# A two-layer decoder trunk on one Trainium2 core: reordering the expert stage's index work, one-hots, four late tiles and gate products

## The chip, the cores and the metric

The kernel runs on one core of a Trainium2 chip. The metric is device time in microseconds (us), from the start to the end of one execution; the profile beside it is one execution of the same program.

## The reference

Two layers. Each has a mixer (a gated linear recurrence beside a sparse attention) and then the PEER expert stage, which the change touches:

```python
q = (xf @ wq).reshape(T, 8, 2, 128)                       # T = 256 tokens, 8 heads
s = jnp.einsum('thcd,ckd->thck', q, subkeys)
sv, si = lax.top_k(s, 16)                                 # top 16 of 128 keys, for both halves
cand = sv[:, :, 0, :, None] + sv[:, :, 1, None, :]        # 16 x 16 sums
cv, ci = lax.top_k(cand.reshape(T, 8, 256), 16)           # top 16 pairs
ea = take_along_axis(si[:, :, 0], ci // 16, axis=-1)
eb = take_along_axis(si[:, :, 1], ci % 16, axis=-1)
experts = ea * 128 + eb                                   # 128 of 16384 experts per token
gate = softmax(cv)
act = gelu(einsum('cd,ced->ce', x, u_tab[experts]))       # rows of 1024
y = einsum('ce,ced->cd', act * gate, v_tab[experts])
x = layer_norm(ALPHA * x + y)
```

## The kernel before

The kernel does not gather rows. It multiplies every token with all 16384 rows of both tables, 128 tiles of 128 rows each, and uses a dense matrix G of gates (128 rows a tile, zero where a token did not choose the expert).

A table tile comes through `wtile` (L95 to L107): SyncE loads 512 KB into `raw` (4 buffers), ScalarE casts it to `hi` (L102, 3 buffers), and VectorE, or GpSimd for the first 14 u tiles (`NPOOL`), takes the remainder `lo` = raw - hi (L103, 3 buffers). TensorE multiplies in three terms, hi·hi, lo·hi and hi·lo. A **u tile** is 24 matmuls (L111); every second one ends in a Gelu on ScalarE into an `act` tile (4 buffers, `NACT`) that is written to DRAM (`kept`). A **v tile** is 12 matmuls (L983).

One layer's expert stage runs through three parts:

- **Index work.** u tiles run on TensorE while VectorE does the top-k. The generator `work()` yields the VectorE cost of each step, and u tiles are put in as that cost adds up. Per head: `query` (a product with wq, copied by ScalarE at L780), scores (L797), `top` (20 VectorE instructions). Per half of the heads (g is 0 or 1): `pairs` (sums `cd`, L811, and their best 16) and `choices` (an Exp on ScalarE, L834, and 26 steps with the tiles `sif`, `ge` and `t` that turn the chosen pairs into indices and gates). `turn_round` transposes the result (L882).
- **One-hots.** 32 steps: two VectorE instructions make one-hot tiles `ohg` for 8 tokens (L934, L938), 16 matmuls (L945) and four ScalarE copies (L949) put their gates into G. The other u tiles lie between.
- **Second pass.** For each pair of v tiles: `fetch` brings an act tile back on SyncE's queue (L965), `w_pair` multiplies it with G on VectorE (L961), `w_split` casts it (ScalarE L974) and takes the remainder (VectorE L975) into `W8`, and the v tiles are multiplied. Near its end, the rows of the layer norm, five or three v tiles and, in the first layer, weights of the next one are loaded ahead.

The framework keeps each engine's queue in order, and its scheduler may move an instruction ahead of program order where its inputs allow; `tc.keep_in_program_order` pins one. The lines to follow are these:

Of the kernel before, what the change touches and what calls it, by code (L numbers as in the profile page):

```python
# [47 lines left out]
ROOT_ACT = {1, 2, 3}  # L48
NACT = 4
NPOOL = 14  # L50
NCAND = 50
CNT = [16 // (i + 1) for i in range(16)]
OFF = [sum(CNT[:i]) for i in range(16)]
# [23 lines left out]
def trunk_kernel(ctx: ExitStack, tc: tile.TileContext, x, xt, cst, lam, pvec, brow, w_in, w_lx, w_v, w_q4, lru_w,  # L77
# [187 lines left out]
    for l in range(NL):  # L265
# [3 lines left out]
        with tc.tile_pool(name="mix", bufs=1, reuse_waits="tile") as mp, \  # L269
# [196 lines left out]
            def gates(qb, br, h0, h1):  # L466
                return vrow[:, qb, 256 + br * 8 + h0:256 + br * 8 + h1]
# [259 lines left out]
        with tc.tile_pool(name="peer", bufs=1, reuse_waits="tile") as pp:  # L727
# [10 lines left out]
            def u_tile(a):  # L738
                if a % 2 == 0:
                    ub[a] = bank()  # L740
                ps = ub[a - a % 2]
                col_mm(ps[:, HALF[a % 2]], wtile(u_tab[l, a], (8, 128), POOL if a < NPOOL else DVE), xT)
                if a % 2:
                    at = act_tile()
                    ACT.activation(at.rearrange("p a b -> p (a b)"), ps, AF.Gelu_apprx_tanh)  # L745
                    kept[a - 1] = spill.tile([128, 2, S], F32, name="kept%d" % (a - 1), bufs=1)
                    ACT.dma_start(kept[a - 1], at)

            with tc.tile_pool(name="topk", bufs=1, reuse_waits="tile") as tk:
# [141 lines left out]
                def work():  # L891
                    for h in (2, 0, 1, 3):
                        yield from top(h)
                    yield from pairs(0)
                    yield from choices(0)
                    for h in range(4, 8):
                        query(h)
                        yield 2.44 - 5.76
                        yield from top(h)
                    yield from pairs(1)  # L900
                    yield from choices(1)
                    yield 0.0
                    yield from turn_round()

                for h in (2, 0, 1, 3):
                    if h == 0:
# [10 lines left out]
            with tc.tile_pool(name="dense", bufs=1, reuse_waits="tile") as dp:  # L917
# [10 lines left out]
                def onehots(t0):  # L928

                    ohg = (state.tile([128, 2, 4, 2, 128, 2], F16, tag="xTf", name="ohg") if t0 % 16 else  # L930
                           pp.tile([128, 2, 4, 2, 128, 2], F16, name="ohg"))
                    oh, og = ohg[:, 0], ohg[:, 1]
                    qs = slice(t0 // 2, t0 // 2 + 4)
                    DVE.tensor_tensor(oh.rearrange("p q w a i -> p (q w) a i"),  # L934
                                      iota.unsqueeze(1).to_broadcast([128, 8, 128, 2]),
                                      eT[:, qs].rearrange("p q w i -> p (q w) i").unsqueeze(2).to_broadcast([128, 8, 128, 2]),
                                      op=ALU.is_equal)
                    DVE.tensor_tensor(og, oh[:, :, 0:1].to_broadcast([128, 4, 2, 128, 2]),  # L938
                                      gT[:, qs].unsqueeze(3).to_broadcast([128, 4, 2, 128, 2]), op=ALU.mult)
                    for h in range(2):  # L940
                        ps = bank()
                        for k in range(4):
                            q, i = divmod(4 * h + k, 2)
                            for w in range(2):
                                PE.matmul(ps[:, k * 128:k * 128 + 128], oh[:, q, 1, :, i], og[:, q, w, :, i],  # L945
                                          start=w == 0, stop=w == 1)
                        t1 = t0 + 4 * h
                        for g in range(2):
                            ACT.activation(G[g][:, :, t1:t1 + 4],  # L949
                                           ps.rearrange("p (t g a) -> p g a t", g=2, a=64)[:, g], AF.Copy, scale=1.0 / GSC)  # L950

                a0 = a
                for i in range(32):
                    onehots(8 * i)
                    while a < 128 and (a - a0) * 32 < (i + 1) * (128 - a0):
                        u_tile(a)
                        a += 1
                assert a == 128

                def w_pair(a0):  # L960
                    DVE.tensor_tensor(act[a0], act[a0], G[a0 // 64][:, a0 % 64:a0 % 64 + 2, :], op=ALU.mult)  # L961

                def fetch(a0):
                    act[a0] = act_tile()
# [87 lines left out]
                for j in range(2):  # L1052
                    ready(j)
                w_pair(body[0])
                for j, p in enumerate(body):
                    ready(j + 2)
                    ready(j + 3)
                    v_tile(p)
                    w_pair(seq[j + 1])
                    v_tile(p + 1)  # L1060
                    step[0] = j
                    left = len(body) - j
                    if left == 16:
                        gb = ln_gb(new_gb, (l, 0))
                        for tb in range(2):
                            ln_affine(gb, tb)
                    if left <= 14 and pre:
                        f, i = pre.pop(0)
                        f(i)
                        if left <= len(pre):  # L1070
                            f, i = pre.pop(0)
                            f(i)
# [193 lines left out]
```

## Time and profile before

| | us |
|---|---|
| median of 3 runs (lowest to highest) | 1985.06 (1984.7 to 1985.13) |
| profiled execution | 1986.41 |
| span of its trace, first to last instruction | 1984.6 |
| TensorE busy in it | 1910.3 (96%) |
| VectorE busy | 1322.8 (67%) |
| ScalarE busy | 976.4 (49%) |
| GpSimd busy | 82.0 (4%) |

The table says which engine has the least idle time over the whole span; it does not say where in the span its idle time lies. PE is TensorE, PEld its weight loads, DVE VectorE, ACT ScalarE, POOL GpSimd, SP SyncE. Most runs of this kernel lie within 0.3% of one another.

### The profile page before, as it was taken

Reading aid. Unit: us, or ns where it says so; the run is one execution under the profiler, and the core shown is the slowest. Engines: PE = TensorE matmul, PEld = TensorE weight load, DVE = VectorE, ACT = ScalarE, POOL = GpSimd, SP = SyncE. Lnnn points to the kernel's source line nnn. Section 1 sums busy time; section 2 is a strip of 40 time slices with the busy share of each in tenths; the row PEclk is TensorE's granted clock in tenths of the full one; section 3 lists DMA queues with packets and bytes.
Section 4 is the critical chain, followed back from the end, with each engine's and each line's share of the span. In section 5 each row is a group of like instructions: output and inputs, shape, how many; then the busy total and the mean of one; then the engine's idle time right before and its main releaser. Section 6 shows DMA issues by size and latency. Waiting matters only on the chain.

```text
span 1984.6 us, 32589 instructions
## 1 busy us (share of the span) xinstructions
PE 1910.3 (96%) x12580; PEld 1681.0 (85%) x12580; DVE 1322.8 (67%) x2553; ACT 976.4 (49%) x1579; POOL 82.0 (4%) x55
## 2 busy tenths in 40 slices
PE   8999899999999999999999998999999989999998
PEld 7858899999998888777868488999999988887876
DVE  5664878666665666657667639786666656667666
ACT  3635444455554555445446344444555545555553
POOL 0005200000000000000000052000000000000000
PEclk9999999999999999999999999999999999999999
DMA  8405547566666777778553056575666657778783
GB/s 276 155 0 180 195 160 234 177 199 207 199 202 215 241 241 242 248 255 278 175 182 106 0 169 188 161 237 175 205 201 203 206 199 254 239 244 264 244 264 117
DMA packets 130096, 393.92 MB, mean 198 GB/s; under 512 B 15634, under 2 KB 16404, under 8 KB 129812
## 3 DMA queue, kind: packets, MB, share of 16 engines
q1 hardware_dynamic: 111508, 358.28, 56.2%
q10 hardware_dynamic: 18432, 33.56, 4.6%
q8 instruction: 98, 1.61, 0.3%
q14 instruction: 58, 0.48, 0.1%
HBM read 357.18 MB, written 34.60 MB: 197 GB/s over the span
## 4 chain that ended last, share of the span: by engine, by line
PE 80%; DMA 9%; DVE 6%; issue 2%; ACT 1%; POOL 0%; SPq 0%; POOLq 0%; DVEq 0%; ACTq 0%
PE ps L111 41%; PE ps L983 25%; DMA act<-kept 6%; PE ps L945 3%; PE ps L589 3%; PE ps L118 2%; DVE lo L103 2%; DMA raw<-in_v_tab_dram 1%; PE ps L231 1%; PE ps L797 1%; PE ps L561 1%; PE ps L514 1%; DVE W L975 1%; PE ps L369 0%; POOL lo L103 0%
## 5 line engine op out<-in xcount | busy, mean ns | idle before, releaser
L102 ACT CAST hi<-raw 128x1024 fp32r<-128x1024 f32 x548 | 575.4, 1051 | 483.5 <-PE ps L111 413.2
L103 DVE TENSOR_TENSOR lo<-raw,hi 128x1024 fp32r<-128x1024 f32 x516 | 629.6, 1222 | 267.3 <-ACT hi L102 266.8
L111 PE MATMUL ps<-xThi,hi 128*128 128x256 f32 x2400 | 692.0, 288 | 6.5 <-ACT hi L102 6.5
L111 PE MATMUL ps<-xThi,lo 128*128 128x256 f32 x2400 | 683.5, 285 | 8.3 <-POOL lo L103 6.0
L111 PE MATMUL ps<-xTlo,hi 128*128 128x256 f32 x2400 | 682.8, 285 | 0.0
L983 PE MATMUL ps<-hi,W 128*128 128x512 f32 x1936 | 523.1, 392 | 10.2 <-ACT W L974 10.0
L111 PEld LDWEIGHTS ps<-xThi,lo 128*128 128x128 f32 x2400 | 463.6, 193 | 10.6 <-POOL lo L103 6.9
L111 PEld LDWEIGHTS ps<-xThi,hi 128*128 128x128 f32 x2400 | 464.1, 193 | 7.9 <-ACT hi L102 6.9
L111 PEld LDWEIGHTS ps<-xTlo,hi 128*128 128x128 f32 x2400 | 464.1, 193 | 0.3
L983 PEld LDWEIGHTS ps<-hi,W 128*128 128x128 f32 x1936 | 365.9, 189 | 88.6 <-ACT W L974 10.4
L983 PE MATMUL ps<-lo,W 128*128 128x512 f32 x968 | 302.6, 394 | 13.1 <-DVE lo L103 12.9
L983 PEld LDWEIGHTS ps<-lo,W 128*128 128x128 f32 x968 | 180.7, 189 | 59.5 <-DVE lo L103 23.2
L974 ACT CAST W<-act 128x256 fp32r<-128x256 f32 x242 | 97.7, 407 | 266.2 <-PE ps L983 258.2
L961 DVE TENSOR_TENSOR act<-act,G 128x512 f32<-128x512 f32 x128 | 88.4, 692 | 172.9 <-DMA act<-kept 170.3
L975 DVE TENSOR_TENSOR W<-act,W 128x256 fp32r<-128x256 f32 x242 | 101.0, 420 | 10.3 <-PE ps L983 8.1
L103 POOL TENSOR_TENSOR lo<-raw,hi 128x1024 fp32r<-128x1024 f32 x32 | 78.5, 2460 | 315.5 <-ACT hi L102 315.5
L949 ACT ACTIVATE G<-ps 128x256 f32<-128x256 f32 x256 | 80.3, 383 | 12.2 <-PE ps L945 8.2
L938 DVE TENSOR_TENSOR ohg<-ohg,gT 128x2048 f16<-128x2048 f16 x64 | 78.2, 1225 | 2.1
L945 PE MATMUL ps<-ohg 128*128 128x128 f16 x1024 | 71.5, 222 | 8.2 <-DVE ohg L938 8.2
L934 DVE TENSOR_TENSOR ohg<-iota,eT 128x2048 f16<-128x2048 f16 x64 | 77.9, 1220 | 1.7 <-PE ps L945 1.7
L745 ACT ACTIVATE act<-ps 128x512 f32<-128x512 f32 x128 | 75.6, 591 | 0.1
L945 PEld LDWEIGHTS <-ohg 128*128 128x128 f16 x1024 | 60.3, 98 | 11.3 <-DVE ohg L938 8.6
(256 smaller groups left out, 1186.6 us busy)
## 6 DMA issues: line engine op xcount, KB each, us to landing
raw<-in_u_tab_dram SPq DMA_DIRECT2D x256, 512.0 KB, 3.6
raw<-in_v_tab_dram SPq DMA_DIRECT2D x256, 512.0 KB, 4.5
kept<-act ACTq DMA_DIRECT2D x128, 256.0 KB, 2.5
act<-kept SPq DMA_DIRECT2D x128, 256.0 KB, 3.8
raw<-in_w_in_dram SPq DMA_DIRECT2D x24, 512.0 KB, 4.3
raw<-in_wq_dram SPq DMA_DIRECT2D x24, 512.0 KB, 4.3
ow<-in_w_out_dram SPq DMA_DIRECT2D x16, 512.0 KB, 7.9
qf<-in_w_q_dram SPq DMA_DIRECT2D x8, 512.0 KB, 3.8
```

The source lines that it names most:

```text
L102: ACT.copy(hi, raw)
L103: lo_eng.tensor_tensor(lo, raw, hi, op=ALU.subtract)
L111: PE.matmul(ps, a[m], b[n], start=start and i == 0, stop=stop and i == 2)
L745: ACT.activation(at.rearrange("p a b -> p (a b)"), ps, AF.Gelu_apprx_tanh)
L934: DVE.tensor_tensor(oh.rearrange("p q w a i -> p (q w) a i"), iota.unsqueeze(1).to_broadcast([128, 8, 128, 2]), eT[:, qs].rearrange("p q w ...
L938: DVE.tensor_tensor(og, oh[:, :, 0:1].to_broadcast([128, 4, 2, 128, 2]), gT[:, qs].unsqueeze(3).to_broadcast([128, 4, 2, 128, 2]), op=ALU. ...
L945: PE.matmul(ps[:, k * 128:k * 128 + 128], oh[:, q, 1, :, i], og[:, q, w, :, i], start=w == 0, stop=w == 1)
L949: ACT.activation(G[g][:, :, t1:t1 + 4], ps.rearrange("p (t g a) -> p g a t", g=2, a=64)[:, g], AF.Copy, scale=1.0 / GSC)
L961: DVE.tensor_tensor(act[a0], act[a0], G[a0 // 64][:, a0 % 64:a0 % 64 + 2, :], op=ALU.mult)
L974: ACT.copy(whi, at[:, a % 2])
L975: DVE.tensor_tensor(wlo, at[:, a % 2], whi, op=ALU.subtract)
L983: PE.matmul(accs[tb * 2 + hf], ww[m][:, TB[tb]], v[n][:, hf * 512:hf * 512 + 512], start=a == first[0] and (m, n) == (0, 0), stop=a == 127 ...
```

## The change

Five edits in the expert stage. In `work()`, `choices(0)` is written after `pairs(1)`, the query of a head is written a head earlier, the costs yielded around them change and the last step yields 4.0 after `turn_round`. The one-hot loop makes the one-hots of a step ahead of the u tiles of the step before, and `gates` (the matmuls and copies) follows them. The last four u tiles (`NLATE`) run after the first two fetches and the first `w_pair` of the second pass. And `w_pair` is pinned to program order.

```diff
--- before.py
+++ after.py
@@ -48,6 +48,7 @@
 ROOT_ACT = {1, 2, 3}
 NACT = 4
 NPOOL = 14
+NLATE = 4
 NCAND = 50
 CNT = [16 // (i + 1) for i in range(16)]
 OFF = [sum(CNT[:i]) for i in range(16)]
@@ -892,15 +893,19 @@
                     for h in (2, 0, 1, 3):
                         yield from top(h)
                     yield from pairs(0)
-                    yield from choices(0)
+                    query(4)
+                    yield 2.44 - 5.76
                     for h in range(4, 8):
-                        query(h)
-                        yield 2.44 - 5.76
+                        if h < 7:
+                            query(h + 1)
+                            yield 2.44 - 5.76
                         yield from top(h)
                     yield from pairs(1)
+                    yield from choices(0)
                     yield from choices(1)
-                    yield 0.0
+                    yield 1.0
                     yield from turn_round()
+                    yield 4.0
 
                 for h in (2, 0, 1, 3):
                     if h == 0:
@@ -937,6 +942,10 @@
                                       op=ALU.is_equal)
                     DVE.tensor_tensor(og, oh[:, :, 0:1].to_broadcast([128, 4, 2, 128, 2]),
                                       gT[:, qs].unsqueeze(3).to_broadcast([128, 4, 2, 128, 2]), op=ALU.mult)
+                    return oh, og
+
+                def gates(t0, oh, og):
+
                     for h in range(2):
                         ps = bank()
                         for k in range(4):
@@ -950,15 +959,18 @@
                                            ps.rearrange("p (t g a) -> p g a t", g=2, a=64)[:, g], AF.Copy, scale=1.0 / GSC)
 
                 a0 = a
+                made = onehots(0)
                 for i in range(32):
-                    onehots(8 * i)
-                    while a < 128 and (a - a0) * 32 < (i + 1) * (128 - a0):
+                    following = onehots(8 * i + 8) if i < 31 else None
+                    while a < 128 - NLATE and (a - a0) * 32 < (i + 1) * (128 - NLATE - a0):
                         u_tile(a)
                         a += 1
-                assert a == 128
+                    gates(8 * i, *made)
+                    made = following
 
                 def w_pair(a0):
-                    DVE.tensor_tensor(act[a0], act[a0], G[a0 // 64][:, a0 % 64:a0 % 64 + 2, :], op=ALU.mult)
+                    i = DVE.tensor_tensor(act[a0], act[a0], G[a0 // 64][:, a0 % 64:a0 % 64 + 2, :], op=ALU.mult)
+                    tc.keep_in_program_order(i)
 
                 def fetch(a0):
                     act[a0] = act_tile()
@@ -1052,6 +1064,8 @@
                 for j in range(2):
                     ready(j)
                 w_pair(body[0])
+                for a in range(128 - NLATE, 128):
+                    u_tile(a)
                 for j, p in enumerate(body):
                     ready(j + 2)
                     ready(j + 3)
```

Where this puts things in the queues can be read at three places. The first is VectorE's queue in the index work of the first layer, before, from the end of the best 16 of `pairs(0)` on; `gt`, `cif`, `ge` and `t1` belong to `choices(0)`, `lo_2106` and `lo_2138` to table tiles:

```order
L833 TENSOR_TENSOR gt_2015<-cv_1363 128x128
L843 CAST cif_2022<-ci_1364 128x128
L850 TENSOR_TENSOR ge_2061<-cif_2022,i16_131 128x2048
L871 TENSOR_REDUCE gs_2016<-gt_2015 128x8
L854 TENSOR_TENSOR t1_2097<-ge_2061,dsi_2020 128x2048
L859 TENSOR_TENSOR t1_2134<-ge_2061,dst_2021 128x2048
L825 TENSOR_TENSOR t1_2097<-t1_2097 128x128x8
L103 TENSOR_TENSOR lo_2106<-raw_2104,hi_2105 128x1024
L825 TENSOR_TENSOR t1_2097<-t1_2097 128x128x4
```

The same place after the change; `lo_2049`, `lo_2082` and `lo_2112` belong to the queries of heads 4 and 5:

```order
L834 TENSOR_TENSOR gt_2784<-cv_1363 128x128
L844 CAST cif_2791<-ci_1364 128x128
L851 TENSOR_TENSOR ge_2833<-cif_2791,i16_131 128x2048
L104 TENSOR_TENSOR lo_2049<-raw_2047,hi_2048 128x1024
L855 TENSOR_TENSOR t1_2866<-ge_2833,dsi_2789 128x2048
L104 TENSOR_TENSOR lo_2082<-raw_2080,hi_2081 128x1024
L826 TENSOR_TENSOR t1_2866<-t1_2866 128x128x8
L860 TENSOR_TENSOR t1_2971<-ge_2833,dst_2790 128x2048
L104 TENSOR_TENSOR lo_2112<-raw_2110,hi_2111 128x1024
```

`choices(0)` still stands right behind `pairs(0)`, since the scheduler brings it forward, and the remainders of two more query tiles stand between its steps. Between its large product (L868 before, L869 after) and the first sum `cd` of the second `pairs` stand the best 16 of four heads and, before, 18 remainders; after the change 5, and the first remainder behind these sums is lo_2550. From the best 16 of `pairs(0)` to lo_2550 there are 11 remainders in all.

The second place is SyncE's queue at the boundary between the passes, before; the act tiles are the fetches for the first v tiles:

```order
L100 DMA raw_7033<-in_u_tab_dram 128x1024
L100 DMA raw_7063<-in_u_tab_dram 128x1024
L100 DMA raw_7113<-in_v_tab_dram 128x1024
L100 DMA raw_7134<-in_v_tab_dram 128x1024
L100 DMA raw_7156<-in_v_tab_dram 128x1024
L100 DMA raw_7177<-in_v_tab_dram 128x1024
L100 DMA raw_7199<-in_v_tab_dram 128x1024
L100 DMA raw_7220<-in_v_tab_dram 128x1024
L965 DMA act_7098<-kept0_1545 128x512
L965 DMA act_7100<-kept2_1638 128x512
L965 DMA act_7103<-kept4_1731 128x512
```

And after the change:

```order
L101 DMA raw_7039<-in_u_tab_dram 128x1024
L101 DMA raw_7069<-in_u_tab_dram 128x1024
L101 DMA raw_7113<-in_v_tab_dram 128x1024
L101 DMA raw_7134<-in_v_tab_dram 128x1024
L977 DMA act_6968<-kept0_1545 128x512
L977 DMA act_6970<-kept2_1638 128x512
L101 DMA raw_7156<-in_v_tab_dram 128x1024
L101 DMA raw_7177<-in_v_tab_dram 128x1024
L101 DMA raw_7199<-in_v_tab_dram 128x1024
L101 DMA raw_7220<-in_v_tab_dram 128x1024
L977 DMA act_7103<-kept4_1731 128x512
```

The first two fetches moved from behind six loads of v tiles to behind two. In the one-hot stage, which is not shown, six u tiles stand on TensorE between `turn_round` and the first one-hot matmuls after the change, and none before.

The third place is VectorE's queue in the second pass, before:

```order
L975 TENSOR_TENSOR W8_7097<-act_7152,W8_7097 128x256
L103 TENSOR_TENSOR lo_7265<-raw_7263,hi_7264 128x1024
L961 TENSOR_TENSOR act_7281<-act_7281,G_3565 128x512
L975 TENSOR_TENSOR W8_7097<-act_7152,W8_7097 128x256
L103 TENSOR_TENSOR lo_7287<-raw_7285,hi_7286 128x1024
L975 TENSOR_TENSOR W8_7097<-act_7195,W8_7097 128x256
L961 TENSOR_TENSOR act_7324<-act_7324,G_3565 128x512
L103 TENSOR_TENSOR lo_7308<-raw_7306,hi_7307 128x1024
L975 TENSOR_TENSOR W8_7097<-act_7195,W8_7097 128x256
L103 TENSOR_TENSOR lo_7330<-raw_7328,hi_7329 128x1024
```

And after the change, at the same tiles:

```order
L972 TENSOR_TENSOR act_7105<-act_7105,G_3661 128x512
L104 TENSOR_TENSOR lo_7222<-raw_7220,hi_7221 128x1024
L987 TENSOR_TENSOR W8_6967<-act_7105,W8_6967 128x256 x2
L104 TENSOR_TENSOR lo_7244<-raw_7242,hi_7243 128x1024
L972 TENSOR_TENSOR act_7152<-act_7152,G_3661 128x512
L104 TENSOR_TENSOR lo_7265<-raw_7263,hi_7264 128x1024
L987 TENSOR_TENSOR W8_6967<-act_7152,W8_6967 128x256 x2
L104 TENSOR_TENSOR lo_7287<-raw_7285,hi_7286 128x1024
L972 TENSOR_TENSOR act_7195<-act_7195,G_3661 128x512
L104 TENSOR_TENSOR lo_7308<-raw_7306,hi_7307 128x1024
```

Before, `w_pair` of act_7281 stood ahead of the splits of act_7195 and act_7238; after, each `w_pair` stands with one remainder between it and its own pair's splits, a pair ahead of that pair's matmuls.

## Rows read from the trace of the kernel before

**Rows 1.** The page: busy times, and the chain that ended last.

```profile
PE 1910.3 (96%) x12580; PEld 1681.0 (85%) x12580; DVE 1322.8 (67%) x2553; ACT 976.4 (49%) x1579; POOL 82.0 (4%) x55
...
PE ps L111 41%; PE ps L983 25%; DMA act<-kept 6%; PE ps L945 3%; PE ps L589 3%; PE ps L118 2%; DVE lo L103 2%; DMA raw<-in_v_tab_dram 1%; PE ps L231 1%; PE ps L797 1%; PE ps L561 1%; PE ps L514 1%; DVE W L975 1%; PE ps L369 0%; POOL lo L103 0%
```

**Rows 2.** The chain: start, length, what held it (a u tile; second pass).

```profile
42.47 2.87 PE ps L111 x24
...
626.05 154.99 PE ps L983 x672
```

**Rows 3.** Ten stretches: length, busy times, granted clock, DMA share, GB/s.

```profile
208.00:340.00 132.00, 122.56 (x994) 120.80 (x993) 109.55 (x345) 59.45 (x70) 3.31 (x1) 0.97 0.60 195
1203.50:1336.00 132.50, 122.93 (x994) 121.27 (x993) 109.44 (x345) 59.45 (x70) 3.31 (x1) 0.97 0.61 195
340.00:353.00 13.00, 8.91 (x61) 8.68 (x60) 8.79 (x10) 3.90 (x7) 0.00 (x0) 0.74 0.34 102
1336.00:1349.00 13.00, 8.92 (x71) 8.68 (x70) 9.93 (x10) 3.90 (x7) 0.00 (x0) 0.87 0.32 103
618.00:632.00 14.00, 9.12 (x43) 7.69 (x42) 7.52 (x12) 4.98 (x9) 0.00 (x0) 0.76 0.73 240
1613.00:1627.00 14.00, 8.85 (x45) 7.50 (x44) 6.87 (x11) 5.47 (x9) 0.00 (x0) 0.88 0.68 239
632.00:785.00 153.00, 153.00 (x677) 126.67 (x676) 105.37 (x140) 82.41 (x113) 0.00 (x0) 1.00 0.72 235
785.00:905.00 120.00, 112.71 (x480) 89.89 (x479) 75.17 (x106) 57.76 (x80) 0.00 (x0) 0.99 0.80 256
905.00:960.00 55.00, 51.74 (x217) 39.71 (x216) 40.05 (x55) 29.04 (x44) 0.00 (x0) 1.00 0.83 275
1790.00:1912.00 122.00, 119.24 (x521) 96.89 (x520) 85.12 (x117) 64.77 (x89) 0.00 (x0) 1.00 0.80 259
```

**Rows 4.** Waits over the whole span: total, times, longest.

```profile
ACT gt L834 <- DVE gt L833: 14.9, 2, 7.4
...
PE ps L945 <- DVE ohg L938: 8.2, 2, 4.1
```

**Rows 5.** Timeline of PE, 256 to 275: start, length, [idle before, releaser].

```profile
259.51 1.16 PE L797 MATMUL ps<-skt,qh 128*128 128x128 f32 x8 [1.50 <-ACT qh L780]
260.42 0.37 PE L111 MATMUL ps<-xThi,hi 128*128 128x256 f32 x1
```

**Rows 6.** Timeline of DVE, 198 to 312.

```profile
203.84 2.49 DVE L842 CAST sif<-si 128x256 f16<-128x256 uint32 x1
...
215.72 3.17 DVE L854 TENSOR_TENSOR t<-ge,dsi 128x2048 f16<-128x2048 f16 x1
...
251.59 0.49 DVE L784 MAX8 sv<-ss 128x8 f32<-128x128 f32 x2 [1.09 <-ACT ss L799]
...
255.63 0.28 DVE L786 MATCH_REPLACE8 s<-sv,ss 128x128 f32<-128x128 f32 x1
...
304.32 0.27 DVE L842 CAST sif<-si 128x256 f16<-128x256 uint32 x1
...
309.71 1.22 DVE L854 TENSOR_TENSOR t<-ge,dsi 128x2048 f16<-128x2048 f16 x1
```

**Rows 7.** Timeline of POOL, 195 to 330.

```profile
214.50 3.31 POOL L103 TENSOR_TENSOR lo<-raw,hi 128x1024 fp32r<-128x1024 f32 x1 [8.32 <-ACT hi L102]
```

**Rows 8.** One stretch more, 204 to 258, columns as in rows 3.

```profile
204.00:258.00 54.00, 47.98 (x381) 47.13 (x379) 45.42 (x136) 22.57 (x28) 5.49 (x2) 0.94 0.56 181
```

**Rows 9.** SyncE's queue, 600 to 640: start, length, what it issued.

```profile
604.18 16.68 SPq L100 DMA_DIRECT2D raw<-in_v_tab_dram  x6
```

**Rows 10.** The page's groups of DVE: busy, mean ns | idle before.

```profile
L103 DVE TENSOR_TENSOR lo<-raw,hi 128x1024 fp32r<-128x1024 f32 x516 | 629.6, 1222 | 267.3 <-ACT hi L102 266.8
...
L961 DVE TENSOR_TENSOR act<-act,G 128x512 f32<-128x512 f32 x128 | 88.4, 692 | 172.9 <-DMA act<-kept 170.3
```

**Rows 11.** DMA issues of the page, KB each, us to landing.

```profile
act<-kept SPq DMA_DIRECT2D x128, 256.0 KB, 3.8
```

## The prediction

> **What bounds the kernel now.** Start with the page. TensorE is busy for 1910.3 of 1984.6 us, and the chain that ended last runs mostly through u tiles (41%) and v tiles (25%) [rows 1]. Busy time on another engine is therefore worth nothing by itself, and the change can win at most what TensorE loses. Next come the unit prices from the chain: a u tile takes 2.87 us, and 672 v matmuls take 154.99, so a v tile of 12 takes 2.77 and a pair 5.54 [rows 2]. The view of stretches then says where the loss lies [rows 3]. In 632 to 785 TensorE is never idle, at full clock, so the middle of the second pass has nothing to give. The other stretches lose time in two ways, idle time and a granted clock under 1.00. For each I take the stretch less PE's busy time, and add (1 - clock) times the busy time, or times the whole stretch where the idle pieces are short:
>
> - Index work, 208 to 340: 132 - 122.56 = 9.4 idle, and 0.03 x 132 = 4.0 of clock, together 13.4. In the second layer 9.6 and 4.0, 13.6.
> - Start of the one-hots, 340 to 353: 4.1 idle and 0.26 x 8.91 = 2.3, together 6.4. Second layer 4.1 and 1.2, 5.3.
> - Boundary of the passes, 618 to 632: 4.9 and 0.24 x 9.12 = 2.2, together 7.1. Second layer 5.15 and 1.1, 6.2.
> - End of the second pass: the undisturbed stretch does 677 matmuls in 153 us, 0.226 each. By that the 480 + 217 from 785 to 960 are worth 157.5 of 175 us, a loss of 17.5, and in the second layer 521 are worth 117.7 of 122, a loss of 4.3.
>
> These sum to 73.8 us. The sums are made against the profiled execution, 1986.41; the median of the runs is 1.35 below it, so I take differences and subtract them from 1985.06. A measurement of this kernel can tell about 0.2% (4 us) from no change.
>
> **A. Index work.** What is to go is a wait for an Exp: ScalarE stood for 7.4 us behind the instruction of VectorE that feeds it, once in each layer [rows 4], with the casts of table tiles queued behind. The two waits of 1.50 us for a copied query (one of them in [rows 5]) go too, since the query comes a head earlier. But the order of the queues shows that `choices(0)` stays where it was and that query remainders now lie between its steps. Behind it the best 16 of all four heads come together, with 5 remainders between them where there were 18. So VectorE becomes the bound. Up to lo_2550 it has the work that it did from 204 to 258, 45.4 us [rows 8], with three more heads. Of a head's 20 instructions, 18 take from 251.59 to 255.91 [rows 6], 4.3 us, so a head takes 4.8 and three take 14.4. Two remainders fewer at 1.22 [rows 10] take off 2.4, and the sums of the second `pairs` add 1.3 (an estimate from their nine short instructions). If GpSimd's remainders do not collide there, `sif` falls from 2.49 to 0.27 and `t` from 3.17 to 1.22 [rows 6], 4.2 less. That makes 54.5. TensorE has until then 13 tiles (two of GpSimd's, and 11 remainders), 37.3 us, four heads' scores at 0.91 (259.51 to 260.42 [rows 5]), 3.6, and some 4 of tiles in hand at 204. It loses 54.5 - 44.9 = 9.6. The collisions can come again, since the last two of GpSimd's remainders now fall among VectorE's products: nothing to 4.2, and I take 2.4, the upper half, because that of 214.50 took 3.31 on GpSimd beside the slow `t` [rows 7]. The clock costs nothing to the 4.0 of before, and I take 2.5, since the waits are shorter but more. That is 14.5 against 13.4 and 13.6: +1.1 and +0.9, **+2**; bounds -3.8 to +4.4 a layer, by the ends of collisions and clock.
>
> The Trainium skill, page "SBUF — State Buffer", section "Who interferes with whom", says that a two-input VectorE instruction on SBUF and a GpSimd instruction that reads SBUF exclude each other for the length of the one that came first. The trace agrees (3.17 against 1.22 us), and the rule speaks against this edit, since it moves GpSimd's last remainders to where VectorE has no slack. By it the sum would take the whole 4.2, some 1.8 more a layer.
>
> **B. One-hots a step ahead.** TensorE waited 4.1 us in each layer for the first one-hots [rows 4]. They depend on the transposes, and now six u tiles (17 us) lie between these and the one-hot matmuls, while the two instructions and the copies take some 4. The wait goes, and no tile is added, since the same 128 are only ordered otherwise. With the clock, 6.4 + 5.3 = 11.7, without it 8.2; I take **-11**, as single short stalls may stay.
>
> **C. Four late tiles.** Before, the first fetch sat in SyncE's queue behind six loads of v tiles that took 16.68 us to go out [rows 9], because they wait for `raw` buffers. Now it sits behind two. It takes 3.8 us to land [rows 11], and the four u tiles give 11.5 us of cover. Product, cast and remainder of the first pair come among the last remainders of u, and are needed only after the fourth tile. With that cover gone the stall would be the one of before. What is late next is the third fetch, still behind four v loads, but its pair starts a pair (5.54 us) later. 7.1 + 6.2 = 13.3, idle time alone 10.0; I take **-12.8**.
>
> **D. Gate products in program order.** VectorE waits 170.3 us in all for `act<-kept` at the product [rows 10]. In the middle this costs nothing (TensorE is full), because the product floats ahead: it asks for a buffer just given up and waits for the whole landing, with v remainders queued behind it. At the end of the pass, where more is loaded, the landings grow and the remainders come late. Pinned, each product comes one pair ahead of its matmuls, with a fetch issued about two pairs (11 us) earlier against 3.8 to land. VectorE is busy for 105.37 of 153 us in the steady stretch, 3.8 of 5.54 a pair, so the in-order queue keeps 1.7 us of slack. What remains is the transfers. From 785 to 960 they carry 120 x 256 + 55 x 275 = 45.8 MB; in 157.5 us this needs 291 GB/s, and the highest mean in these rows is 275 [rows 3]. At 275 the stretch takes 166.7, a loss of 9.2 in place of 17.5; if 291 is met, none. I take the middle, 4.5, a gain of 13. In the second layer 31.6 MB in 117.7 us need 268, less than 275 and close to it: I leave 1.3, a gain of 3. **-16**; bounds -8.3 - 1.3 = -9.6 and -21.8.
>
> **Sum.** +2 - 11 - 12.8 - 16 = -37.8: 1948.6 for an execution like the profiled one, **1947 us** against the median. All bounds together give 1931 and 1967.
>
> **The rivals.**
>
> 1. *Transfers are no limit at the end* (D whole, -21.8). For it: the mean of 275 GB/s includes pauses in which the queue waited for buffers. Against it: the landing time is already what VectorE waits for. 1985 + 2 - 11 - 12.8 - 21.8 = 1941; with the lower bound of A, 1932. The Trainium skill, page "DMA: Bandwidth & Descriptors", section "Where 436 GB/s comes from", puts the HBM limit of one core at about 358 GB/s. By that 291 would be met and this rival would hold; no row here is above 275.
> 2. *Index work gets worse.* Every collision returns and the clock drops more often, +4.4 to +8 a layer: 1954 to 1961. For it: rows 8 and the bunched heads; against it: no wait for the Exp holds the casts any more.
> 3. *The end of the pass is a matter of transfers alone* (D nothing): 1963. For it: the DMA share is 0.80 to 0.83 there [rows 3]. Against it: TensorE is full in a stretch at 0.72, so the step between is small.
> 4. *The pinned product uses up the lead* (slower). With one pair of lead, a late fetch stops the product, the splits and the remainder of its own pair, and TensorE with them. D then gains nothing, and over the 121 pairs of both layers the 21.8 us that A to C gain are eaten from 0.18 us a pair on; it decides where fetches land later than the 11 us of their lead. Against it: 3.8 to land. At half a microsecond a pair 1985 - 21.8 + 60 = 2024.
>
> That the change does not do what it says holds for `choices(0)`, which is in the forecast.
>
> **How the numbers follow.** The forecast 0.50; rival 1 0.20; rival 2 0.16; rival 3 0.09; rival 4 0.05. The range 1933 to 1964 leaves out the far ends of rivals 1 and 2 and rival 4, under 2 in 10. Faster by over 0.2%: 0.95; rival 4 is split into 0.02 within it and 0.03 slower.
>
> **What will show it.** ScalarE's wait for `gt` gone, and waits of TensorE for the remainders of u tiles between 220 and 262 in its place (A). No idle time of TensorE ahead of the first one-hot matmuls (B), nor ahead of the first v tile, with the first fetch issued before the last u tile ends (C). VectorE's 170 us of waiting for `act<-kept` down to a few tens, and PE idle after 785 only where GB/s is highest (D). The prediction is wrong if TensorE waits for the product or the split in the middle of the second pass, or if the index stretch loses more than 18 us.

## The result and the profile after

The changed kernel takes 1938.22 us (median of 4 runs, 1935.71 to 1939.46) against 1984.98 in the same comparison, a ratio of 0.9763 with a 95% interval of 0.9746 to 0.9780: 46.8 us faster. The forecast was 1947, range 1933 to 1964. The span of the profiled execution went from 1984.6 to 1936.5.

The page of the changed kernel, its busy times, the chain that ended last, and the two groups that answer to [rows 10]:

```profile
PE 1894.0 (98%) x12580; PEld 1679.2 (87%) x12580; DVE 1330.6 (69%) x2553; ACT 966.3 (50%) x1579; POOL 83.1 (4%) x55
...
PE ps L112 39%; PE ps L995 34%; PE ps L954 3%; PE ps L119 3%; PE ps L590 3%; DVE lo L104 1%; PE ps L562 1%; DMA raw<-in_v_tab_dram 1%; PE ps L515 1%; DVE si L789 1%; DVE cd L812 1%; PE ps L232 1%; DVE s L787 1%; DVE si L786 0%; DVE t L866 0%
...
L104 DVE TENSOR_TENSOR lo<-raw,hi 128x1024 fp32r<-128x1024 f32 x516 | 635.1, 1232 | 396.4 <-ACT hi L103 396.0
...
L972 DVE TENSOR_TENSOR act<-act,G 128x512 f32<-128x512 f32 x128 | 87.5, 685 | 6.6 <-DMA act<-kept 6.6
```

TensorE is busy for less time than before (1894.0 against 1910.3 in [rows 1]) with the same number of instructions. Fewer matmuls ran at the lower clock (mean granted clock 0.991 against 0.987), and matmuls that stand in a stall count as busy too: from 785 to 960 before, 695 of them were busy for 164.45 us, where 0.226 each makes 157.1. In the chain `act<-kept` is no longer among the lines shown; it had 6%. VectorE's wait for it at the product fell from 170.3 us to 6.6. Its wait for ScalarE's casts rose (396.0 against 266.8); from 600 to 960, where TensorE is now full, it went from 21.4 to 83.6, so there it costs nothing.

What the product's wait did to TensorE shows in the page's group for the matmuls that use a v tile's remainder `lo`, first before, then after (behind the bar: busy us, mean ns; then the idle time in front of them):

```profile
L983 PE MATMUL ps<-lo,W 128*128 128x512 f32 x968 | 302.6, 394 | 13.1 <-DVE lo L103 12.9
L995 PE MATMUL ps<-lo,W 128*128 128x512 f32 x968 | 298.1, 389 | 0.2 <-DVE lo L104 0.2
```

The stretches that answer to [rows 3] and [rows 8], in the same columns (length, PE, PEld, DVE, ACT, POOL busy, clock, DMA share, GB/s):

```profile
204.00:258.00 54.00, 48.38 (x378) 47.77 (x376) 53.97 (x218) 23.92 (x29) 6.38 (x2) 0.94 0.50 156
208.00:340.00 132.00, 123.15 (x987) 122.74 (x988) 106.97 (x313) 58.10 (x69) 6.38 (x2) 0.96 0.62 196
1171.70:1304.00 132.30, 122.28 (x981) 121.66 (x981) 106.44 (x313) 57.97 (x69) 6.32 (x2) 0.96 0.63 193
340.00:358.00 18.00, 18.00 (x153) 18.00 (x152) 13.04 (x14) 7.77 (x9) 0.00 (x0) 1.00 0.68 217
600.00:616.00 16.00, 16.00 (x136) 15.66 (x135) 9.39 (x12) 9.16 (x16) 0.00 (x0) 1.00 0.63 219
1565.00:1581.00 16.00, 16.00 (x136) 15.62 (x135) 9.30 (x12) 9.26 (x16) 0.00 (x0) 1.00 0.68 220
773.00:930.00 157.00, 156.84 (x693) 129.54 (x692) 118.56 (x157) 85.33 (x121) 0.00 (x0) 1.00 0.87 292
1747.00:1869.00 122.00, 122.00 (x540) 101.03 (x539) 92.14 (x125) 65.94 (x93) 0.00 (x0) 1.00 0.84 270
```

By the prediction's own measure (idle time, and the clock's share) the index work loses 8.85 + 0.04 x 132 = 14.1 us in the first layer and 10.0 + 5.3 = 15.3 in the second. (The clock stands in these rows to two digits, so each clock term can be off by 0.7.) The start of the one-hots (340 to 358, and 1304 to 1322 in the second layer) and both boundaries (600 to 616, 1565 to 1581) lose nothing, with TensorE busy throughout. At the end of the second pass, by 0.226 us a matmul, 693 of them are worth 156.6 of 157, and 540 are worth 122 of 122.

| Term | forecast, us | measured, us | of which |
|---|---|---|---|
| A, index work | +2 | +2.4 | 14.1 - 13.4, 15.3 - 13.6 |
| B, one-hots ahead | -11 | -11.7 | 6.4 and 5.3 gone |
| C, late tiles | -12.8 | -13.3 | 7.1 and 6.2 gone |
| D, products in order | -16 | -21.4 | 17.5 to 0.4, 4.3 to 0 |
| Sum | -37.8 | -44.0 | |

The medians differ by 46.8, 2.8 more than these terms, and the two profiled executions (1986.41 and 1938.31), from which the terms are read, by 48.1, 4.1 more. Some 1.1 of it lies in the mixers, which the change does not touch (the matmuls of the first end at 162.6 in place of 163.2); no stretch shown here holds the rest.

In the index work, the waits of TensorE and the wait of ScalarE that answers to [rows 4], 190 to 345:

```profile
PE ps L112 <- DVE lo L104: 8.9, 3, 4.0
...
ACT gt L835 <- DVE gt L834: 4.2, 1, 4.2
```

TensorE now waits three times for a remainder from VectorE, 8.9 us in all: 2.7 at 210.7, behind the best 16 of `pairs(0)`, 2.2 at 236.5 and 4.0 at 261.3. The wait for the Exp did not go, it is 4.2 long; but TensorE does not wait for it. On VectorE's timeline two instructions stand out, 225.24 and 236.55:

```profile
225.24 4.50 DVE L866 TENSOR_TENSOR t<-cif,i 128x2048 f16<-128x2048 f16 x1
...
235.21 1.22 DVE L104 TENSOR_TENSOR lo<-raw,hi 128x1024 fp32r<-128x1024 f32 x1
236.55 3.22 DVE L104 TENSOR_TENSOR lo<-raw,hi 128x1024 fp32r<-128x1024 f32 x1
```

and on GpSimd's, over the same time:

```profile
224.75 2.85 POOL L104 TENSOR_TENSOR lo<-raw,hi 128x1024 fp32r<-128x1024 f32 x1 [22.17 <-ACT hi L103]
235.15 3.54 POOL L104 TENSOR_TENSOR lo<-raw,hi 128x1024 fp32r<-128x1024 f32 x1 [7.55 <-ACT hi L103]
```

The product of 2.28 us takes 4.50 and a remainder of 1.22 takes 3.22, each while GpSimd makes the remainder of u tile 12 or 13, which itself takes 2.85 and 3.54. VectorE is busy for 53.97 of the 54 us from 204 to 258.

At the boundary, SyncE's queue and the chain:

```profile
597.38 4.19 SPq L101 DMA_DIRECT2D raw<-in_v_tab_dram  x2
601.62 0.90 SPq L977 DMA_DIRECT2D act<-kept  x2
604.12 9.94 SPq L101 DMA_DIRECT2D raw<-in_v_tab_dram  x4
```

```profile
597.91 3.96 PE ps L112 x33
601.87 0.94 PE ps L954 x16
602.80 11.56 PE ps L112 x96
614.36 15.67 PE ps L995 x69
```

Two v loads go out at 597.4 and 601.2, then the fetches at 601.62, and the chain passes from the u tiles (the 96 matmuls are the four late ones) to the v tiles without a step between. Before, the chain held the fetch there:

```profile
615.37 2.82 PE ps L111 x23
...
620.91 3.86 DMA act<-kept
```

### The profile page after: what moved, and what is told of

It reads as the page before. It is cut to its first block, busy times and chain, and to the rows that moved or that the text cites. A ratio compares the mean times of both kernels' runs of the same rounds, so it can differ in the third digit from the quotient of the medians.

```text
span 1936.5 us, 32461 instructions
## 1 busy us (share of the span) xinstructions
PE 1894.0 (98%) x12580; PEld 1679.2 (87%) x12580; DVE 1330.6 (69%) x2553; ACT 966.3 (50%) x1579; POOL 83.1 (4%) x55
## 4 chain that ended last, share of the span: by engine, by line
PE 88%; DVE 8%; DMA 2%; issue 1%; ACT 1%; SPq 0%; POOL 0%; DVEq 0%; ACTq 0%; POOLq 0%
PE ps L112 39%; PE ps L995 34%; PE ps L954 3%; PE ps L119 3%; PE ps L590 3%; DVE lo L104 1%; PE ps L562 1%; DMA raw<-in_v_tab_dram 1%; PE ps L515 1%; DVE si L789 1%; DVE cd L812 1%; PE ps L232 1%; DVE s L787 1%; DVE si L786 0%; DVE t L866 0%
## 5 line engine op out<-in xcount | busy, mean ns | idle before, releaser
L104 DVE TENSOR_TENSOR lo<-raw,hi 128x1024 fp32r<-128x1024 f32 x516 | 635.1, 1232 | 396.4 <-ACT hi L103 396.0
L995 PE MATMUL ps<-hi,W 128*128 128x512 f32 x1936 | 517.8, 389 | 0.0
L995 PE MATMUL ps<-lo,W 128*128 128x512 f32 x968 | 298.1, 389 | 0.2 <-DVE lo L104 0.2
```

The source lines that it names most:

```text
L104: lo_eng.tensor_tensor(lo, raw, hi, op=ALU.subtract)
L995: PE.matmul(accs[tb * 2 + hf], ww[m][:, TB[tb]], v[n][:, hf * 512:hf * 512 + 512], start=a == first[0] and (m, n) == (0, 0), stop=a == 127 ...
```

## The experiments

The runs of the kernel before lay between 1982.4 and 1995.2 in these comparisons, so a few microseconds are read from the stretches of the profile and not from the medians. A loss is reckoned as above: idle time and the clock's share, or in the second pass the stretch less 0.226 us a matmul.

**1. The pin alone.** The kernel before, with

```diff
-DVE.tensor_tensor(act[a0], act[a0], G[a0 // 64][:, a0 % 64:a0 % 64 + 2, :], op=ALU.mult)
+i = DVE.tensor_tensor(act[a0], act[a0], G[a0 // 64][:, a0 % 64:a0 % 64 + 2, :], op=ALU.mult)
+tc.keep_in_program_order(i)
```

> The kernel before with one edit, w_pair pinned to program order. Theory 'separate terms' (each edit removes its own loss, and the losses add): the end of the second pass loses nothing more, -17 us in the first layer and -4 in the second, so 21 us less than before, 1964, with the stalls of index work, one-hot start and boundary where they were. Rival 'shared lead' (the pinned product pays only because the late tiles give the fetches a head start): TensorE waits for the products from the boundary on, and the gain is under 10 us, 1975 or more.

Measured: 1960.29 us, ratio 0.985 (0.9825 to 0.9874), which is 29 us under the median of the kernel before in the same comparison (1989.67). The span of its trace is 1963.3, 21 less than before. The end of the second pass in both layers:

```profile
780.00:935.00 155.00, 154.48 (x680) 127.08 (x679) 116.31 (x155) 83.39 (x118) 0.00 (x0) 1.00 0.86 286
1757.00:1912.00 155.00, 155.00 (x685) 128.34 (x684) 115.51 (x155) 83.00 (x118) 0.00 (x0) 1.00 0.82 265
```

680 matmuls are worth 153.7 of 155, and 685 are worth 154.8. The pin alone removes the loss of the end of the pass (1.3 and 0.2 left of 17.5 and 4.3), and the idle time in front of the `lo` matmuls goes from 13.1 to 0.5. The boundary still stalls (618 to 632: TensorE busy for 9.13 of 14). So the rival "shared lead" falls: the product pays without the late tiles.

**2. All but the pin.** The changed kernel without these lines.

> The changed kernel without the pin. Separate terms: the 21 us at the end of the second pass come back, 1959 in all, and the boundary stays closed. Shared lead: without the pin the products float ahead at the boundary too and stop VectorE there, so more than 28 us come back, over 1966.

Measured: 1950.94 us, ratio 0.9815 (0.9788 to 0.9842); 12.7 above the changed kernel, not 21 and not 28. The wait is there again at its old size (172.8 us):

```profile
L972 DVE TENSOR_TENSOR act<-act,G 128x512 f32<-128x512 f32 x128 | 88.5, 692 | 173.2 <-DMA act<-kept 172.8
```

but TensorE loses only 5.7 and 5.8 us at the end of the pass (163 less 696 x 0.226, 155 less 660 x 0.226), and the idle time in front of the `lo` matmuls is 7.4, not 13.1:

```profile
767.00:930.00 163.00, 159.53 (x696) 129.41 (x695) 114.76 (x158) 87.36 (x121) 0.00 (x0) 1.00 0.83 281
1740.00:1895.00 155.00, 151.25 (x660) 122.91 (x659) 109.08 (x150) 82.22 (x113) 0.00 (x0) 1.00 0.77 253
```

So both theories missed. The boundary stayed closed, as separate terms said (600 to 616: TensorE busy for all 16 us), but the loss from a floating product is no fixed sum. Over the layers of three kernels without the pin it was 17.5 and 4.3 (before), 5.7 and 5.8 (here), and 16.6 and 6.5 (experiment 6). What sets the size each time was not found.

**3. No late tiles.** `NLATE = 4` becomes `NLATE = 0`.

> The changed kernel with NLATE = 0, so that the first fetch is again behind six loads of v tiles. Separate terms: the stall of the boundary comes back, 7.4 + 6.7 = 14 us, 1952. Rival 'the pin closes the boundary too' (the first products no longer crowd VectorE there): less than 5 us comes back, under 1943.

Measured: 1953.35 us, ratio 0.9815 (0.9791 to 0.9839), 15.1 above the changed kernel. Boundary and end of the first layer's pass:

```profile
606.00:622.00 16.00, 12.09 (x82) 10.81 (x80) 6.92 (x10) 7.50 (x18) 0.00 (x0) 0.80 0.74 258
773.00:930.00 157.00, 155.52 (x684) 127.83 (x683) 116.91 (x155) 84.46 (x119) 0.00 (x0) 1.00 0.86 284
```

3.9 idle and 0.20 x 12.09 = 2.4 of clock come back at the boundary, 6.3 a layer, and 2.4 at the end of the pass (157 less 684 x 0.226). The second layer is alike (1582 to 1598: 4.0 idle and 0.19 x 12.01 = 2.3). Separate terms hold; the pin does not close the boundary.

**4. The old order of the index work.** In the changed kernel:

```diff
                     yield from pairs(0)
-                    query(4)
-                    yield 2.44 - 5.76
+                    yield from choices(0)
                     for h in range(4, 8):
-                        if h < 7:
-                            query(h + 1)
-                            yield 2.44 - 5.76
+                        query(h)
+                        yield 2.44 - 5.76
                         yield from top(h)
                     yield from pairs(1)
-                    yield from choices(0)
                     yield from choices(1)
```

> The changed kernel with the old order in work() (choices(0) before the second heads, each query just ahead of its scores), but with the new yields around turn_round, so that the one-hots stay ahead. Separate terms: the bunched heads cost 0.7 and 1.3 us more than the Exp's wait did, so this kernel is 2 us faster than the changed one, 1936. Rival 'the index edits gain' (what was saved at the Exp and the queries is more than what the heads cost): 5 us slower or more, 1943.

Measured: 1937.7 us (1933.11 to 1939.67), ratio 0.9732 (0.9705 to 0.976). TensorE's waits in the index work are those of before again, for queries and for the table tiles behind the Exp:

```profile
PE ps L798 <- ACT qh L781: 3.0, 2, 1.5
PE ps L112 <- POOL lo L104: 2.9, 1, 2.9
PE ps L112 <- ACT hi L103: 1.1, 1, 1.1
```

With one of 0.4 for a remainder from VectorE they sum to 7.4 us where the changed kernel had 8.9. The stretch of the first layer:

```profile
208.00:340.00 132.00, 124.64 (x1004) 122.96 (x1004) 106.93 (x318) 60.87 (x72) 3.31 (x1) 0.97 0.62 196
```

It loses 7.4 + 4.0 us; the second layer (1174.6 to 1306.9, TensorE busy for 123.03, clock 0.97) loses 9.3 + 4.0. That is 24.7 in both where the changed kernel loses 29.4, and 2.2 of the difference is idle time alone. The edit to `work()` gains nothing: the rival falls. The medians cannot tell the 2 us of the other side; the stretches show some 2 to 5.

**5. One-hots not ahead.** The one-hot loop and the costs around `turn_round` as before.

```diff
-                made = onehots(0)
                 for i in range(32):
-                    following = onehots(8 * i + 8) if i < 31 else None
+                    gates(8 * i, *onehots(8 * i))
...
-                    gates(8 * i, *made)
-                    made = following
```

> The changed kernel with the old one-hot loop (one-hots made just ahead of their matmuls) and the old costs around turn_round. Separate terms: TensorE waits again 4.1 us for the first one-hots and runs some matmuls at the lower clock, 7 and 6 us of loss at that place, 1938 + 12.5 = 1950. Rival 'the later tiles cover it' (u tiles ahead of the first one-hots come from the scheduler anyway): under 4 us, below 1942.

Measured: 1951.92 us, ratio 0.9827 (0.9807 to 0.9846), 13.7 above the changed kernel. The first layer's start of the one-hots shows the wait and the clock of before (3.5 idle, 0.74), and the second layer's (1311 to 1324) 4.1 idle at 0.74, so 5.9 and 6.4 us lost:

```profile
340.00:353.00 13.00, 9.54 (x67) 9.54 (x68) 8.18 (x9) 3.18 (x8) 0.00 (x0) 0.74 0.26 93
```

**6. A fifth act buffer.** The kernel before with `NACT = 5`.

> The kernel before with five act buffers in place of four, and nothing pinned. The order of the queues shows the product floating four pairs ahead instead of three. Theory 'float' (an unpinned product always asks for the buffer that was given up last, however many there are, and stops VectorE for a landing): the loss at the end of the second pass stays over 12 us in the first layer, 1985 give or take 6. Rival 'too few buffers' (one more gives the fetches time): that loss falls below 5 us, 1972 or less.

Measured: 1987.06 us, ratio 1.0 (0.9987 to 1.0014). The end of the pass loses 175 - 158.4 = 16.6 and 122 - 115.5 = 6.5:

```profile
785.00:960.00 175.00, 165.51 (x701) 129.40 (x701) 117.05 (x163) 89.47 (x130) 0.00 (x0) 1.00 0.80 263
1790.00:1912.00 122.00, 118.08 (x511) 94.81 (x509) 82.99 (x113) 64.85 (x89) 0.00 (x0) 1.00 0.76 253
```

VectorE waits 185.9 us for `act<-kept` at the product, and the idle time in front of the `lo` matmuls is 14.7. So it was not too few buffers. With one more the product floats one pair further and asks again for the buffer given up last; with experiment 1, which changes the order alone, the cause of the stall is the order.

**7. `choices` kept where it is written.** In the changed kernel:

```diff
-                    DVE.tensor_tensor(gt, cv[:, g], cv[:, g, :, 0:1].to_broadcast([128, 8, 16]), op=ALU.subtract)
+                    i = DVE.tensor_tensor(gt, cv[:, g], cv[:, g, :, 0:1].to_broadcast([128, 8, 16]), op=ALU.subtract)
+                    tc.keep_in_program_order(i)
...
-                    DVE.tensor_copy(sif, si[:, g])
-                    DVE.tensor_copy(cif, ci[:, g])
+                    for dst_, src_ in ((sif, si), (cif, ci)):
+                        i = DVE.tensor_copy(dst_, src_[:, g])
+                        tc.keep_in_program_order(i)
```

> The changed kernel with the first three VectorE instructions of choices pinned to program order, so that choices(0) runs behind the second pairs, where it is written. Theory 'bunching' (VectorE is the bound of the index work because choices(0) floats ahead of the four heads): up to the remainder behind the second sums VectorE has 54 - 13 = 41 us of work against 45 of TensorE, so the loss of 14.6 and 15.7 us falls to 4 to 6 a layer, 1938 - 19 = 1919. Rival 'total work' (VectorE is short over the whole index stretch, so that the waits only move behind the second pairs): the loss stays within 3 us, 1935 or more.

Measured: 1922.5 us (1920.19 to 1925.28), ratio 0.9673 (0.9651 to 0.9696), 15.7 less than the changed kernel. The two stretches of the index work:

```profile
204.00:258.00 54.00, 50.08 (x405) 49.67 (x405) 43.36 (x228) 21.93 (x27) 4.80 (x2) 0.97 0.53 168
208.00:340.00 132.00, 128.15 (x1053) 127.68 (x1054) 110.48 (x321) 62.44 (x75) 4.80 (x2) 0.99 0.65 206
```

VectorE is busy for 43.36 of 54 us, not 53.97, and over the stretch TensorE loses 3.85 + 1.3 = 5.2 us, not 14.1. Of the 10.6 us that VectorE no longer does here, 4.2 are the collisions: GpSimd's two remainders (at 224.44 and 234.85) now take 2.40 each, since the products of `choices(0)` have moved away from them (the 4.50 is 2.28 again, at 280.26). The other 6.4 are work that is done later. Bunching holds: without the floating `choices(0)` VectorE is no longer full. How much of the gain is the collisions' share is not told apart here. The longest wait left is for the first remainder of head 4's query, behind the best 16 of `pairs(0)`:

```profile
210.34 0.58 PE L112 MATMUL ps<-xThi,lo 128*128 128x256 f32 x1 [2.63 <-DVE lo L104]
```

**8. More remainders on GpSimd.** The changed kernel with `NPOOL = 20`.

> The changed kernel with the remainders of six more u tiles (14 to 19) on GpSimd. Bunching: they fall beside the best 16 of the second heads, where VectorE is full; 6 x 1.2 us less work there, 7 us less loss a layer if GpSimd does not slow those instructions, 1924. Rival 'port' (a remainder on GpSimd holds up VectorE for about 2 us whenever a two-input product meets it, 4.50 us in place of 2.28 in the changed kernel): the six collide as the last two do, 2 us each, 4 us a layer worse, 1946.

Measured: 1953.18 us, ratio 0.9828 (0.9809 to 0.9847), 15 slower than the changed kernel. On VectorE's timeline:

```profile
226.41 4.50 DVE L866 TENSOR_TENSOR t<-cif,i 128x2048 f16<-128x2048 f16 x1
...
236.39 3.33 DVE L104 TENSOR_TENSOR lo<-raw,hi 128x1024 fp32r<-128x1024 f32 x1
...
246.26 2.42 DVE L826 TENSOR_TENSOR t<-t 128x512 f16<-128x512 f16 x1
...
249.33 2.64 DVE L828 TENSOR_TENSOR ev<-t 128x128 f32<-128x128 f16 x1
```

Four instructions are about 2 us longer than elsewhere (2.28, 1.22, 0.42 and 0.40 us). The first two are so in the changed kernel too; the last two are new, beside GpSimd's remainders at 245.79 and 249.25. The port rival is right in kind. It was too small, since a second thing comes in that neither named: ScalarE's wait for `gt` is longer, up to 9.0 us, with casts of table tiles queued behind it, and TensorE now waits for such a cast:

```profile
ACT gt L835 <- DVE gt L834: 13.2, 2, 9.0
...
PE ps L112 <- ACT hi L103: 5.8, 1, 5.8
```

**9. Fewer remainders on GpSimd.** The changed kernel with `NPOOL = 12`.

> The changed kernel with the remainders of u tiles 12 and 13 on VectorE in place of GpSimd. Theory 'port' (those two held VectorE up by 2.2 and 2.0 us in the changed kernel, 4.50 in place of 2.28 and 3.22 in place of 1.22): no instruction of VectorE there is lengthened any more, it does 2.4 us of remainders itself instead of 4.2 us of being held, so the index work loses 1.8 us less in each layer, 1934.5. Rival 'help' (GpSimd's remainders are work taken off a full VectorE): 2.4 us more in each layer, 1943.

Measured: 1937.58 us (1934.67 to 1939.62), ratio 0.9749 (0.9729 to 0.9769). The product is at its 2.29 us again, and GpSimd has nothing in the stretch:

```profile
225.06 2.29 DVE L866 TENSOR_TENSOR t<-cif,i 128x2048 f16<-128x2048 f16 x1
```

```profile
204.00:258.00 54.00, 47.75 (x373) 47.35 (x372) 52.80 (x217) 22.99 (x28) 0.00 (x0) 0.94 0.50 159
```

VectorE is still busy for 52.80 of 54 us. The time is that of the changed kernel within what the runs can tell, so "help" (1943) falls. By the stretches (208 to 340: busy 123.68; 1174.1 to 1306.4: 123.73; both at 0.96) the loss is 13.6 and 13.9 for 14.1 and 15.3, so 1.9 us are gained where "port" had 3.6; that is close to what the rounding of the clock leaves open. The collision is seen to go; most of the loss stays.

**10. Query 4 earlier.** Kernel 7 with `query(4)` and its yield ahead of `pairs(0)`.

> The kernel with the pinned choices, and query(4) written ahead of pairs(0). What is left of the loss there (7.0 us a layer) begins with 2.8 us in which TensorE waits for the first remainder of query(4), which stands behind the best 16 of pairs(0). Theory 'bunching': with that remainder ahead, this wait and the matmuls at the lower clock behind it go, 3 to 4 us a layer, 1922 - 7 = 1915. Rival 'total work': the wait comes back at the next remainder behind pairs(0), no change, 1922 give or take 2.

Measured: 1928.43 us, ratio 0.9706 (0.9685 to 0.9727), 6 slower than kernel 7. The wait came back at the next remainder behind `pairs(0)`, and longer, 4.32 for 2.63:

```profile
214.84 0.58 PE L112 MATMUL ps<-xThi,lo 128*128 128x256 f32 x1 [4.32 <-DVE lo L104]
```

The stretch from 208 to 340 loses 5.8 + 4.0 us, not 5.2. The rival is right that the wait moves on; that it would grow was in neither. (The expectation reckons with 7.0 us a layer left in kernel 7; by the measure used here it is 5.2.)

**11. Query 4's remainders on GpSimd.** Kernel 7 with `POOL if h < 5` in place of `POOL if h < 4` in `query`.

> The kernel with the pinned choices (query(4) back behind pairs(0)), and the two remainders of head 4's query on GpSimd in place of VectorE. Theory 'order' (the 2.8 us at 207 is only the wait for VectorE's queue, which stands at the best 16 of pairs(0), and GpSimd does not lengthen those one-input instructions): the wait goes, with the matmuls at the lower clock behind it, 3 to 4 us a layer, 1922 - 7 = 1915. Rival 'moves on' (as in the kernel before this one, the wait comes back at the next query's remainder on VectorE): within 3 us of 1922.

Measured: 1915.36 us (1914.52 to 1916.82), ratio 0.9634 (0.9618 to 0.965), the fastest of all kernels here:

```profile
208.00:340.00 132.00, 130.48 (x1087) 130.03 (x1087) 111.93 (x333) 64.63 (x76) 6.10 (x3) 1.00 0.67 208
```

TensorE is busy for 130.48 of 132 us at full clock, and the longest wait left is 1.3. "Order" holds: the wait was for the place in VectorE's queue, and it does not move on.

## Why the prediction came out as it did

**What bounds the kernel: right.** All but 3 to 4 us of what the change gained lay in the four places found from the idle time and the clock, and the middle of the second pass gave nothing.

**A: right in sign and sum, with parts wrong that cancel.** The order of the queues said that `choices(0)` would not move back and that VectorE would be the bound, and it is (53.97 of 54). Experiment 4 shows that the edit's index part gains nothing, and 7 that most of the loss comes from the floating `choices(0)` and the collisions that it brings; the 2.6 us wait that is left there, for the query written earlier, goes in 11. The prediction took 2.4 us for the collisions; the changed kernel has 2.2 + 2.0 = 4.2, the whole of the upper bound. The Trainium skill, page "SBUF — State Buffer", section "Who interferes with whom", excludes two such instructions from each other for a whole instruction's length, and here the trace agrees with the rule and not with my half. But TensorE is idle for 8.9 us in the first layer, collisions and all, not for 9.6 + 2.4, and the clock took 5.3, not 2.5, over the 4.0 that was given as its bound: the first was set too high by what the second was set too low, and that the sum fits is luck. What made the first too high is VectorE's work up to lo_2550: it begins that remainder at 259.99, 56.0 us after 204, and without the 4.2 of collisions that is 51.8, where the prediction summed 54.5. The wait for the Exp is not gone (4.2 us), only covered.

**B and C: right.** -11.7 for -11 and -13.3 for -12.8; each comes back when it is undone alone (13.7 us in experiment 5; 15.1 in 3, of which 2 at the end of the pass).

**D: right in mechanism, too small.** The step that failed is the middle taken between "no limit" and "275 GB/s": the changed kernel moves 292 GB/s on average from 773 to 930 with TensorE full, over the 291 that the sum asked for. Rival 1 (1941) was the true case. So the row of 275 was no bound of the transfers; it was a mean over a stretch with stalls, in which TensorE was idle for 3.3 of 55 us. Why it was not higher is argued, not shown: with TensorE late, `raw` buffers come free late and the queue pauses. The Trainium skill's figure for a core, about 358 GB/s (page "DMA: Bandwidth & Descriptors", section "Where 436 GB/s comes from"), pointed that way; that 358 can be reached no run here shows. Experiments 1 and 6 confirm the cause (order, not buffers). Experiment 2 limits it: at the end of the pass the pin is worth 20.3 us on the kernel before and 11.1 on the changed one (12.7 by the medians), so the terms do not add for this edit.

**Rivals 2, 3 and 4** did not come: index work lost 15.3 at most, the end of the pass lost nothing, and no product stopped TensorE in the middle. (The outer bounds of the sum add up to 1931 and 1966, not 1967.)

**Open.** Why a floating product costs 4 us in one layer and 17 in another; what the collisions cost TensorE by themselves (experiment 9 takes them away but puts their remainders on VectorE, 1.8 us less a layer in all); and 2 to 3 us of the gain.

## What to carry to other kernels

Writing an instruction later does not make it run later where a scheduler may bring it forward: read the order of the queues, and pin the few instructions that head the chain. An instruction that asks for a buffer just given up stops its whole in-order queue for a landing, and a further buffer does not help if the scheduler floats it again. A mean rate of transfers taken from a stretch with stalls is no limit for a kernel without them: 275 GB/s before, 292 after.

## What the runs showed of the hardware

In a collision of VectorE and GpSimd one waits for the other. VectorE's instruction became some 2 us longer whatever its own length, one of 0.4 us (2.42, 2.64) as one of 2.28 (4.50). GpSimd's remainder of 2.40 became 2.85 and 3.54 where one instruction of VectorE was under way when it began (a remainder from 224.11 on) or began with it, and a second one followed: the 1.22 us remainder at 235.21 kept its length and the one at 236.55 took 3.22. Where only one fell into it, GpSimd's was not lengthened (2.34 at 236.30 in experiment 8, beside VectorE's 3.33 at 236.39).

The best-16 instructions were not lengthened: in kernel 11 they take 0.19 to 0.22 us beside a remainder on GpSimd from 204.02 on, those that read two tiles in their rows too (MATCH_REPLACE8 c<-cv,cd, 0.20), so the "one-input" of its expectation is not what the rows show. That fits that two remainders moved to GpSimd beside them gained in experiment 11. In experiment 8 six more went there; the first two met products of `choices(0)`, and the three from 253.06 on ran beside the best 16 of a head, which kept their 0.27 to 0.29 us.
